# Forgetting attention on one core: softmax sums taken from the transposed weights in heads 0 to 12

## The chip, the cores and the metric

One core of a Trainium2 chip. The metric is device time in microseconds for one execution of the whole program, the median of several runs.

## The reference

Two residual layers and a final RMS norm over x of 1024 positions by 1024 channels, in float32. Layer 0 is a gated linear recurrence (RG-LRU). Layer 1, which the change touches, is attention with a forget gate, 16 heads of 64 channels, in blocks of 128 queries:

```
logits = jnp.einsum("bqhd,bkhd->bhqk", q_blk, kf) * scale
logits = logits + (cq_blk[..., :, None] - ck[:, :, None, :])
logits = jnp.where(mask[None, None], logits, NEG_INF)
p = jax.nn.softmax(logits, axis=-1)
return jnp.einsum("bhqk,bkhd->bqhd", p, vf)
```

`cum` (above `cq_blk` and `ck`) is the running sum of log-sigmoids of the forget logits. The result is multiplied by a SiLU gate and projected out.

## The kernel before

**Number format.** Every float32 product is made of three TensorE matmuls on a high and a low part (`to_hi`, `to_lo`, lines 75 to 86): the high part is the value rounded to the type of TensorE's faster float32 mode, the low part the rest. The helpers `gemm_steps` (lines 111 to 113) and `weights` do this for all projections.

**Stages.** Up to about 460 us layer 0 runs: projections, convolution, scan, output projection. Then the 16 heads of layer 1 follow one another in the loop of line 910. The projections that a later pair of heads needs (queries and keys by `kq_units`, gates by `g_units`, values by `values`) and, from head 13 on, the output projection (`partial`) serve as `fill`: single steps of them are put between the steps of the attention, so that TensorE has work while the others prepare its operands.

**One head.** Queries are treated in two halves of 512 columns, c = 0 and 1. Two generators work on a head:

- `maxima(hd, c)` makes the logits with queries on the partitions, one block of 128 queries after another, in the PSUM tile S (two buffers of two banks). Each stretch of columns takes two matmuls that accumulate: line 656 with the mixed high and low parts (128 rows), line 657 with 96 rows that hold one product of the parts and the forget sums. VectorE adds the causal mask and takes the row's negative maximum in one instruction (line 661); ScalarE takes the exponential in place and its row sum (line 664). The maxima are transposed (L668) and written as four rows of the operand U (L669).
- `weigh(hd, c)` makes the logits again, transposed, with keys on the partitions (lines 723 and 724, tile ST with the same PSUM tag as S); the maxima are now already in the operands, so ScalarE's exponential (729, 732) gives the weights `p`. GpSimd zeroes what the causal mask forbids (737), VectorE splits `p` into `ph` and `pl` (helper lines 81 and 86), and TensorE multiplies them by the values into O (757, 758). ScalarE and VectorE fold the two halves of O into `yo` (762, 763).

After the second half of `maxima` the sums are doubled, inverted and transposed (680 to 685), written to DRAM (686) and read back, spread over 64 partitions, as `recb` (690). `scale(hd)` multiplies the gate by it on GpSimd (699). For odd heads `gated(hd, c)` multiplies `yo` of the pair by that (772), and stores it (778), to be read again (808) as the input of the output projection.

**Order.** The function `run` goes through a string: a digit takes the next step of `weigh` (0) or `maxima` (1), a dot a step of the fill. The first string of a head joins `weigh(hd, 0)` with `maxima(hd, 1)`, the second `weigh(hd, 1)` with `maxima(hd + 1, 0)`:

```
run(first, weigh(hd, 0), maxima(hd, 1), fill=fill, side=side)
scale(hd)
gated(hd, 0)
run(second, weigh(hd, 1), maxima(hd + 1, 0), fill=fill, side=side)
gated(hd, 1)
```

The order in the source is a priority: the planner (`schedule_with_timeline_sim`) plays the program through once at build time and fixes from it the order on each engine's queue, SP's DMA queue among them. On the chip each queue goes in that order. Line 938 loads the operands T and U of head hd + 2 by eight DMAs (`load`: six for the parts of queries and keys, of which the change exchanges two sources, and two for the forget sums).

Tiles come from pools with few buffers: `p`, `ph`, `pl` and `yo` have two, `recb` one, the tag `xp` three (used by the loads of `y` and by `partial`), the PSUM tag O two (O itself, the transposed maxima and the transposed sums).

## Time and profile before

| | |
|---|---|
| time, three runs | 1174.61, 1177.04, 1177.36 us; median 1177.04 |
| the profiled execution | 1181.24 us; its span 1179.5 us |
| TensorE matmuls busy | 1145.0 us, 97% |
| VectorE busy | 830.9 us, 70% |
| ScalarE busy | 594.7 us, 50% |
| GpSimd busy | 404.4 us, 34% |
| mean granted TensorE clock | 0.981 |

All times of instructions come from the one profiled execution. The span is from its first to its last instruction. Busy shares are averages over stages with different limits; a busy TensorE is not TensorE at its peak, as the records of successive matmuls overlap. What a matmul costs in a stream is the distance from its start to the next one's. In a row of instructions, `S<-T,U` says that tile S is written from T and U, and the time in brackets is idle time of the engine before the row, with what ended it.

### The profile page before, as it was taken

What the parts mean: (1) busy time and instruction counts of PE and PEld (TensorE: products, weight loads), DVE (VectorE), ACT (ScalarE), POOL (GpSimd) and SP (SyncE); (2) the same over time, 40 slices, a digit from 0 to 9 for tenths busy, and PEclk for the clock granted to TensorE, in tenths of its full rate; (3) what the DMA queues carried; (4) which work ended last, traced back from release to release, by engine and by line L of the source; (5) the groups of instructions that cost most, each with busy time, mean ns of one, the idle gap of its engine ahead of it and who ended that gap; (6) DMA issues with size and microseconds to landing.
All of it is one profiled execution on the core that took longest, in us unless ns stands there. A gap on an engine that the chain in (4) does not pass through costs nothing.

```text
span 1179.5 us, 15836 instructions
## 1 busy us (share of the span) xinstructions
PE 1145.0 (97%) x5653; PEld 958.7 (81%) x5653; DVE 830.9 (70%) x1272; ACT 594.7 (50%) x1010; POOL 404.4 (34%) x367
## 2 busy tenths in 40 slices
PE   8998999999999999999999999999999999998996
PEld 7786888888888877978888988789888898786895
DVE  7588946766567679666877767777577775675766
ACT  8277453454543757354554545445454454435343
POOL 1223333333323332332343332333333233234345
PEclk8999999999999999999999999999999999998996
DMA  6111111111112214541343413433234332756434
GB/s 207 50 41 31 59 45 46 53 49 41 54 32 59 63 45 138 133 120 56 91 117 75 106 63 91 118 84 88 63 90 109 91 82 61 194 151 199 139 117 143
DMA packets 63278, 105.95 MB, mean 90 GB/s; under 512 B 8856, under 2 KB 27928, under 8 KB 63200
## 3 DMA queue, kind: packets, MB, share of 16 engines
q1 hardware_dynamic: 63200, 104.95, 31.9%
q8 instruction: 44, 0.72, 0.3%
q14 instruction: 34, 0.28, 0.1%
HBM read 63.30 MB, written 16.45 MB: 68 GB/s over the span
## 4 chain that ended last, share of the span: by engine, by line
PE 81%; DVE 9%; DMA 3%; ACT 3%; issue 2%; POOL 1%; SPq 0%; DVEq 0%; ACTq 0%; POOLq 0%
PE gps L111 10%; PE gps L112 10%; PE gps L113 10%; PE ops L113 5%; PE ops L111 5%; PE ops L112 4%; PE ups L111 4%; PE ups L113 4%; PE ups L112 4%; PE ST L723 3%; PE O L758 3%; PE ST L724 3%; PE O L757 2%; PE S L657 2%; PE S L656 2%; PE vps L519 2%
## 5 line engine op out<-in xcount | busy, mean ns | idle before, releaser
L86 POOL TENSOR_TENSOR wl<-wf,wh 128x512 fp32r<-128x512 f32 (+2 forms) x154 | 223.6, 1458 | 409.1 <-ACT wh L75 370.0
L111 PE MATMUL gps<-hh,wh 128*128 128x512 f32 x576 | 227.2, 395 | 0.7 <-DVE qkl L557 0.7
L113 PE MATMUL gps<-hl,wh 128*128 128x512 f32 x576 | 227.1, 394 | 0.0
L112 PE MATMUL gps<-hh,wl 128*128 128x512 f32 x576 | 227.1, 394 | 0.0
L75 ACT CAST wh<-wf 128x512 fp32r<-128x512 f32 (+2 forms) x156 | 93.4, 606 | 118.6 <-PE gps L113 34.1
L664 ACT ACTIVATE S<-S,st 128x128 f32<-128x128 f32 (+7 forms) x128 | 91.4, 714 | 113.6 <-DVE st L661 106.4
L81 DVE CAST ph<-p 128x512 fp32r<-128x512 f32 (+2 forms) x130 | 87.1, 680 | 61.6 <-ACT p L729 31.6
L113 PEld LDWEIGHTS gps<-hl,wh 128*128 128x128 f32 x576 | 108.7, 189 | 24.3 <-issue 0.2
L111 PEld LDWEIGHTS gps<-hh,wh 128*128 128x128 f32 x576 | 108.9, 189 | 21.9 <-DVE qkl L557 1.1
L112 PEld LDWEIGHTS gps<-hh,wl 128*128 128x128 f32 x576 | 108.9, 189 | 21.5 <-POOL wl L86 0.3
L737 POOL TENSOR_SCALAR_AFFINE_SELECT p<-p 128x128 f32<-128x128 f32 (+1 forms) x128 | 48.0, 393 | 203.4 <-ACT p L732 104.2
L86 DVE TENSOR_TENSOR pl<-p,ph 128x512 fp32r<-128x512 f32 (+2 forms) x130 | 115.1, 902 | 2.3
L661 DVE CUSTOM_DVE_ANT_0 S<-S,mask 128x128 f32<-128x128 f32 (+7 forms) x128 | 96.6, 758 | 6.7 <-PE S L657 5.7
L351 DVE TENSOR_TENSOR x<-x,ops 128x512 f32<-128x512 f32 x80 | 53.6, 681 | 41.5 <-PE ops L113 41.3
L111 PE MATMUL ups<-hh,wh 128*128 128x512 f32 x192 | 77.9, 406 | 4.0 <-ACT hh L77 2.0
L113 PE MATMUL ups<-hl,wh 128*128 128x512 f32 x192 | 77.3, 403 | 0.1
L112 PE MATMUL ups<-hh,wl 128*128 128x512 f32 x192 | 77.0, 401 | 0.0
L729 ACT ACTIVATE p<-ST 128x512 f32<-128x512 f32 (+1 forms) x68 | 53.1, 786 | 44.2 <-PE ST L724 39.0
L519 PE MATMUL vps<-wh,hh 128*128 128x256 f32 (+1 forms) x256 | 72.9, 286 | 0.2 <-DVE qkl L557 0.2
L521 PE MATMUL vps<-wl,hh 128*128 128x256 f32 (+1 forms) x256 | 72.5, 285 | 0.4 <-POOL wl L86 0.4
L520 PE MATMUL vps<-wh,hl 128*128 128x256 f32 (+1 forms) x256 | 72.8, 285 | 0.0
L656 PE MATMUL S<-T,U 128*128 128x256 f32 (+2 forms) x192 | 68.5, 359 | 2.8 <-ACT S L664 2.8
(193 smaller groups left out, 2633.9 us busy)
## 6 DMA issues: line engine op xcount, KB each, us to landing
wf<-in_w SPq DMA_DIRECT2D x100, 256.0 KB
wf<-in_wo SPq DMA_DIRECT2D x64, 128.0 KB
T<-qkh SPq DMA_DIRECT2D x28, 256.0 KB
U<-qkh SPq DMA_DIRECT2D x28, 256.0 KB
x<-in_xt SPq DMA_DIRECT2D x16, 256.0 KB
x1d<-x SPq DMA_DIRECT2D x16, 256.0 KB
wf<-in_wv SPq DMA_DIRECT2D x16, 256.0 KB
xp<-x1d SPq DMA_DIRECT2D x16, 256.0 KB
```

Of the source, the lines that this page charges most:

```text
L75: nc.scalar.copy(hi, src)
L81: eng.tensor_copy(hi, src)
L86: return eng.tensor_tensor(lo, src, f32(hi), ALU.subtract)
L111: nc.tensor.matmul(o, wh, xh[:, cs], start=i == 0, stop=False)
L112: nc.tensor.matmul(o, wl, xh[:, cs], start=False, stop=False)
L113: nc.tensor.matmul(o, wh, xl[:, cs], start=False, stop=i == len(pairs) - 1)
L519: nc.tensor.matmul(pt, xh, wh, start=k == 0, stop=False)
L520: nc.tensor.matmul(pt, xl, wh, start=False, stop=False)
L521: nc.tensor.matmul(pt, xh, wl, start=False, stop=k == KT - 1)
L656: nc.tensor.matmul(S[:, lo_:hi_], U[s][:, 0, qs], T[s][:, 0, lo_:hi_], start=True, stop=False)
L661: nc.vector.tensor_tensor_reduce(S[:, :n], S[:, :n], mask[:, SEQ - n :], -1.0, -NEG, ALU.add, ALU.min, accum_out=m)
L664: nc.scalar.activation(S[:, :n], S[:, :n], AF.Exp, bias=f32(m), scale=-1.0, accum_out=sums[:, i : i + 1])
```

## The change

For heads 0 to 12 (`hd < LIGHT`):

- `maxima` makes only the second of its two matmuls. `load` exchanges the low and the high part of the queries in U, so that this one now holds the product of the high parts with the forget sums. The maximum of these rougher logits is only a shift that cancels between weights and sums.
- The exponential of the untransposed logits and its row sum go.
- `weigh` adds up the masked weights `p` over the blocks of keys in an accumulator `acc` on VectorE (tag `xp`), and at the end of each half four float32 matmuls with a column of ones sum it over the partitions; VectorE copies the four columns to the place where ScalarE's sums stood.
- The inversion of the sums (now the function `inverse`) comes after the second half of `weigh`, and `scale` and `gated(hd, 0)` come after the second `run`.

For all heads the high part of `p`, where no column of the step is masked, is now made by ScalarE instead of VectorE.

```
-                nc.sync.dma_start(f32(A[:64, 0, cs]), hi)
+                nc.sync.dma_start(f32(A[:64, 0, cs]), hi if is_k else lo)
...
-                    nc.sync.dma_start(f32(A[:64, 1, cs]), lo)
+                    nc.sync.dma_start(f32(A[:64, 1, cs]), hi)
...
-                    nc.tensor.matmul(S[:, lo_:hi_], U[s][:, 0, qs], T[s][:, 0, lo_:hi_], start=True, stop=False)
                     last[0] = nc.tensor.matmul(
-                        S[:, lo_:hi_], U[s][:96, 1, qs], T[s][:96, 1, lo_:hi_], start=False, stop=True
+                        S[:, lo_:hi_], U[s][:96, 1, qs], T[s][:96, 1, lo_:hi_], start=True, stop=light
                     )
+                    if not light:
+                        last[0] = nc.tensor.matmul(
+                            S[:, lo_:hi_], U[s][:, 0, qs], T[s][:, 0, lo_:hi_], start=False, stop=True
+                        )
...
-                nc.scalar.activation(S[:, :n], S[:, :n], AF.Exp, bias=f32(m), scale=-1.0, accum_out=sums[:, i : i + 1])
+                if not light:
+                    nc.scalar.activation(
+                        S[:, :n], S[:, :n], AF.Exp, bias=f32(m), scale=-1.0, accum_out=sums[:, i : i + 1]
+                    )
...
+            if not light and (hd == HEADS - 1 or c == 1):
+                inverse(hd, 4 * c if hd == HEADS - 1 else 0, 4 * c + 4)
...
+            acc = at.tile([P, HALF], F32, tag="xp", name="acc", bufs=3) if hd < LIGHT else None
...
-                    to_hi(ph[:, sl, :n], p[:, sl, :n], nc.vector)
+                    to_hi(ph[:, sl, :n], p[:, sl, :n], nc.vector if masked else nc.scalar)
...
+                if acc is not None:
+                    d = [q - begin for q in qlo]
+                    if j0 == 0:
+                        if d[1]:
+                            nc.vector.tensor_copy(acc[:, : d[1]], p[:, 0, : d[1]])
+                        nc.vector.tensor_tensor(acc[:, d[1] :], p[:, 0, d[1] :], p[:, 1, : ns[1]], ALU.add)
+                    else:
+                        for jj in range(2):
+                            a_ = acc[:, d[jj] :]
+                            nc.vector.tensor_tensor(a_, a_, p[:, jj, : ns[jj]], ALU.add)
...
+            if acc is not None:
+                col = ps.tile([P, HALF], F32, tag="O", name="sums")[:, :4]
+                for b in range(4):
+                    nc.tensor.matmul(
+                        col[:, b : b + 1], acc[:, b * P : (b + 1) * P], onesf[:, :1], start=True, stop=True
+                    )
+                nc.vector.tensor_copy(stats[hd][1][:, 4 * c : 4 * c + 4], col)
+                if c == 1:
+                    inverse(hd, 0, 8)
+                yield
...
-            scale(hd)
-            gated(hd, 0)
+            if hd >= LIGHT:
+                scale(hd)
+                gated(hd, 0)
             run(second, weigh(hd, 1), maxima(hd + 1, 0), fill=fill, side=side)
             drain(side)
+            if hd < LIGHT:
+                scale(hd)
+                gated(hd, 0)
             gated(hd, 1)
```

40 lines of the change are left out of this document (22 added, 18 removed).

## The prediction

> **What bounds the kernel now.** I read the page first (busy shares, the chain of waits), then the windows by stage, then the timelines of single engines.
>
> ```profile
> span 1179.5 us, 15836 instructions
> ...
> PE 1145.0 (97%) x5653; PEld 958.7 (81%) x5653; DVE 830.9 (70%) x1272; ACT 594.7 (50%) x1010; POOL 404.4 (34%) x367
> ...
> PE 81%; DVE 9%; DMA 3%; ACT 3%; issue 2%; POOL 1%; SPq 0%; DVEq 0%; ACTq 0%; POOLq 0%
> ```
>
> TensorE (PE) is busy for 97% of the span and holds 81% of the chain that ended last; VectorE (DVE) is next with 70% and 9%. ScalarE (ACT), from which the change takes most work, holds 3% of the chain. These are averages, so the stage of heads 0 to 12 is looked at by itself (columns: window, its length, then busy us of PE, weight loads, DVE, ACT and POOL, granted clock, DMA share, GB/s):
>
> ```profile
> 553.00:972.00 419.00, 415.64 (x2249) 358.21 (x2248) 308.51 (x578) 209.99 (x430) 146.53 (x162) 1.00 0.36 90
> 583.00:615.00 32.00, 31.14 (x154) 26.01 (x153) 25.73 (x46) 17.30 (x36) 14.82 (x15) 1.00 0.47 115
> 615.00:646.00 31.00, 30.94 (x153) 25.79 (x152) 24.62 (x45) 15.87 (x32) 8.69 (x12) 1.00 0.34 79
> ```
>
> From 553 to 972 us PE is idle for 3.4 us of 419 (419.00 less 415.64), at full granted clock. DVE has 74% of this stage (308.51 of 419), and 79 to 80% in heads where no value projection dilutes it (24.62 of 31, 25.73 of 32). So in this stage time is the sum of PE's start-to-start intervals. ACT is idle for 46 to 50% of it (17.30 of 32 busy, 209.99 of 419), and taking work from it gives nothing by itself.
>
> **Change, term 1: the pass of untransposed logits that goes (PE).** The form of each row below: start, duration, instruction. A matmul's slot is the distance to the next start, since durations overlap.
>
> ```profile
> 597.48 0.28 PE L656 MATMUL S<-T,U 128*128 128x256 f32 x1
> 597.60 0.29 PE L657 MATMUL S<-T,U 96*128 96x256 f32 x1
> ...
> 602.38 0.40 PE L656 MATMUL S<-T,U 128*128 128x512 f32 x1
> 602.62 0.40 PE L657 MATMUL S<-T,U 96*128 96x512 f32 x1
> 602.85 0.34 PE L656 MATMUL S<-T,U 128*128 128x384 f32 x1
> 603.03 0.34 PE L657 MATMUL S<-T,U 96*128 96x384 f32 x1
> ```
>
> A slot is 0.235 us for 512 columns (602.38 to 602.85 is two), 0.18 for 384 (602.85 to 603.03), 0.12 for 256 (597.48 to 597.60); I estimate 0.15 for 320, between the last two. By the loop of `maxima` a head has five matmuls of 512 in a pass, two of 384, two of 320 and three of 256: 1.175 + 0.36 + 0.30 + 0.36 = 2.2 us. For 13 heads: 28.5 us less on PE.
>
> **Term 2: the sums of the transposed weights that come (PE).** Each half of a head gets four matmuls of one column, with a 128x128 block of the float32 accumulator as weights. The norm's column sums have this form already:
>
> ```profile
> 458.09 1.84 PE L133 MATMUL sscol<-onesf,sq 128*128 128x1 f32 x16
> 459.80 0.48 PE L111 MATMUL gps<-hh,wh 128*128 128x512 f32 x1
> 460.11 0.40 PE L425 MATMUL ops<-yh,wh 128*128 128x512 f32 x1
> ```
>
> In the code that is eight matmuls (four blocks, two parts), and the row has 16 records, two for each. They hold PE for 1.71 us (458.09 to 459.80), 0.107 us a record, although each has one column to stream: their price is not their width. The matmul behind them takes a slot of 0.31 us and not 0.235, 0.08 more. A group of four is thus 8 x 0.107 + 0.08 = 0.935 us, and 26 groups (13 heads, two halves) come to 24.3 us. Terms 1 and 2 leave PE with only 4.2 us less.
>
> The Trainium skill ("TensorE: Matmul & The Clock Gate", section "LDWEIGHTS") puts a weight load at columns over 1.2 GHz, an estimate of 107 ns for 128, and the row agrees to the nanosecond. The same page's section "Back-to-back issue gap" gives a matmul of 1 to 64 columns about 25 ns, by which the 208 records would cost an estimated 5 us; the row, with a new weight for every record, speaks against that.
>
> **Term 3: VectorE and ScalarE (off PE's path, if they stay under it).**
>
> ```profile
> L664 ACT ACTIVATE S<-S,st 128x128 f32<-128x128 f32 (+7 forms) x128 | 91.4, 714 | 113.6 <-DVE st L661 106.4
> ```
> ```profile
> L86 DVE TENSOR_TENSOR pl<-p,ph 128x512 fp32r<-128x512 f32 x69 | 50.7, 735 | 1.5
> L81 DVE CAST ph<-p 128x1024 fp32r<-128x1024 f32 x30 | 41.2, 1374 | 31.0 <-ACT p L729 31.0
> L664 ACT ACTIVATION_READ_ACCUMULATOR S<-S,st 128x1 f32 x128 | 24.8, 194 | 0.1
> L75 ACT CAST xch<-xc 128x1024 fp32r<-128x1024 f32 x12 | 12.6, 1050 | 54.3 <-DVE xc L265 54.3
> L685 DVE COPY rc<-tr 8x128 f32<-8x128 f32 x15 | 4.2, 277 | 10.7 <-PE tr L683 10.7
> ```
>
> ACT loses eight exponentials a head with their accumulator reads, 8 x (0.714 + 0.194) = 7.3 us, and gets two casts of 1024 columns, 2 x 1.05 = 2.1 us. DVE gets ten adds a head over 3,840 columns in all (896 in the first half, 2,944 in the second); at the 0.735 us of a 512-column subtraction of the same kind that is 5.5 us, and with three small copies at 0.277 it is 6.3 us. It loses two casts at 1.374, 2.75 us. Net it gains 3.6 us a head, so 25.73 becomes 29.3 of 32 us and 24.62 becomes 28.2 of 31: 91%. It stays under PE, and the adds are urgent for nobody but the two-buffer tile `p` and the end of the half, so I cost them at nothing on the path; without that cover it is 3.6 us a head less the 6.3 us of idle DVE time. The logit tile S leaves its PSUM buffer after the maximum instead of after the exponential, which helps PE. PE's own waits between 535 and 985 us (sum, times, longest):
>
> ```profile
> PE O L758 <- DVE pl L86: 3.2, 3, 1.3
> ```
> ```profile
> PEld ST L723 <- ACT S L664: 1.7, 7, 0.3
> ```
>
> They are three for `pl`, 3.2 us together, and the weight loads' queue waited 1.7 us for S, held by ScalarE. The three `pl` waits have a cause that the change moves:
>
> ```profile
> 588.75 2.39 POOL L699 TENSOR_TENSOR sg<-sg,recb 64x1024 f32<-64x1024 f32 x1 [3.55 <-ACT yo L762]
> 591.22 1.62 POOL L86 TENSOR_TENSOR wl<-wf,wh 128x512 fp32r<-128x512 f32 x1
> 592.80 2.27 POOL L772 TENSOR_TENSOR yo<-yo,sg 128x512 f32<-128x512 f32 x1
> 595.02 1.43 POOL L737 TENSOR_SCALAR_AFFINE_SELECT p<-p 128x128 f32<-128x128 f32 x4
> ```
> ```profile
> 586.57 1.22 DVE L86 TENSOR_TENSOR pl<-p,ph 128x1024 fp32r<-128x1024 f32 x1
> ...
> 591.73 2.20 DVE L86 TENSOR_TENSOR pl<-p,ph 128x1024 fp32r<-128x1024 f32 x1
> ```
>
> The same subtraction takes 1.22 us with GpSimd idle and 2.20 us beside its 591.22 and 592.80. Now the scaling moves out of the half with the widest tiles, so I take half of the 3.4 us of idle PE as gained: 1.7, between nothing and all of it. The Trainium skill ("SBUF — State Buffer", section "SBUF: two separate sides") states that a DVE instruction with two SBUF inputs and a reading GpSimd instruction exclude each other on a shared port pair. The 2.20 agrees in kind, and by that rule the ten adds would also hold up the masks.
>
> **Term 4: what moves.** For heads 0 to 12 the reciprocal, its two DMAs, `scale` and the first `gated` (with its store) go from the middle of the head to its end, ahead of the load of head hd+2 on SP's queue and of the next head's masks on POOL's. Scale and two gated products are 2.39 + 2.27 + 2.27 = 6.9 us of POOL in a row at the end of an odd head. I cost this at nothing because PE has projection matmuls there; the rival below prices the loss of that cover. The reordered high and low parts in `load` are the same eight DMAs: nothing.
>
> **Term 5: the accumulators share the buffers "xp"**, which before were free until head 13, so that three loads of `y` went out early:
>
> ```profile
> 604.06 0.34 SPq L808 DMA_DIRECT2D y<-y1d  x1
> ...
> 1008.73 9.03 SPq L808 DMA_DIRECT2D y<-y1d  x6
> ```
> ```profile
> 1014.25 0.62 ACT L75 CAST yhh<-y 128x512 fp32r<-128x512 f32 x1 [4.51 <-DMA y<-y1d]
> ```
>
> A load costs the queue 1.5 us (9.03 over 6) and ScalarE already waits 4.51 us for one. Between none and three of them (4.5 us) become late; I take one, +1.5 us, as the last accumulator of head 12 is the only one held to the end.
>
> **Sum.** -28.5 + 24.3 - 1.7 + 1.5 = -4.4 us, against the profiled execution of 1181.24 us, 1.7 above its own span and 4.2 above the median of 1177.04. From the median: 1172.6 us. A measurement of this kernel tells about 0.3%, 3.5 us, from no change, so the forecast stands just beyond that.
>
> **Rivals.**
>
> *GpSimd's end-of-head chain stalls PE (slower).* If the next head's masks stand behind scale and gated in POOL's order while these wait for the reciprocals, the splits and then the output matmuls come late at each of 13 transitions. By the row of three waits one costs 1.07 us: 13.9 us, and with terms 1, 2 and 5 it is 1177.0 - 2.7 + 13.9 = 1188 us. It decides once the chain from column sum to masks is longer than the projection work beside it. A wait near 2 us costs double:
>
> ```profile
> 1023.80 0.50 PE L723 MATMUL ST<-U,T 128*128 128x512 f32 x1 [1.90 <-ACT S L664]
> ...
> 1026.14 0.63 PE L112 MATMUL ops<-yhh,wl 128*128 128x512 f32 x1
> 1026.57 0.63 PE L113 MATMUL ops<-yhl,wh 128*128 128x512 f32 x1
> ```
>
> Behind that wait the slots are 0.43 us (1026.14 to 1026.57) for a while, at half the speed. For it: waits for the reciprocals end much of POOL's idle time. Against: the same chain in the middle of the head cost PE three waits in twelve heads.
>
> *DVE becomes the bound (slower).* If the adds meet GpSimd as the 2.20 us row does, 5.5 us a head becomes 9.9 (x 1.8), and 24.62 + 3.6 + 4.4 = 32.6 us exceeds the 31 of the head. In seven even heads that is 1.6 us each, 11 us, and 1184 us after term 1 and 2. Against: GpSimd is busy for only 8.69 us of those 31.
>
> *All idle time goes (faster).* S is free earlier and ACT is nearly empty: -4.2 - 3.4 = -7.6, 1169.4 us; if the wait at 1023.80 with its slow slots (1.9 + about 2) is replanned away too, 1165.5.
>
> *The cheap sums (faster).* If the sums' weight loads hid under the neighbouring matmuls they would cost next to nothing: up to 28.5 us, 1149. The 16 records in a row with 0.107 each speak against it; the skill's 25 ns sentence above is its only support.
>
> *It gives nothing.* A tile S that takes half as long to make waits for DVE's maximum, and the 4.2 us come back as such waits: 1177.
>
> **How the numbers follow.** Forecast (PE's difference decides, ends from -8 to 0 us): 0.50. POOL chain 0.17, DVE 0.10, nothing gained 0.08, idle time gone 0.12, cheap sums 0.03. Faster by over 0.3% (under 1173.5): 0.31 of the forecast's 0.50, with 0.12 and 0.03: 0.46. Slower (over 1180.6): most of 0.17 and 0.10, 0.24. The rest, 0.30, within. Range: from 1165 (idle time gone) to 1187 (just short of the POOL chain in full); 2 in 10 outside. The likeliest case's own range is 1169 to 1177.
>
> **What would show it.** Right: 156 fewer matmuls at the S line, 208 more records of one column at 0.107 us slots in groups of eight; DVE near 84% from 553 to 972 us (308.5 + 12 x 3.6 over 419), ACT near 35% (210.0 - 12 x 5.2); PE's idle time in that stage no greater than 3.4 us. Wrong: output or column-sum matmuls waiting for DVE by 1 us and more at the ends of heads; masks on POOL that follow scale and gated immediately; a half-speed stretch inside heads 0 to 12; column sums at slots under 0.05 us.

## The result, and the profile after

The changed kernel takes 1196.63 us, the median of four runs (1194.78 to 1199.61), beside 1177.2 us of the kernel before (four runs, 1174.61 to 1178.74): a ratio of 1.0168, with a 95% interval from 1.0145 to 1.019. It is slower by 19.4 us, where 4.4 less was forecast, and it lies above the predicted range, which ended at 1187 us. Its profiled execution took 1196.33 us, 15.1 more than the profiled one of before.

The page of the changed kernel: span, busy shares, the chain that ended last, and the group of adds.

```profile
span 1194.6 us, 15842 instructions
...
PE 1143.5 (96%) x5705; PEld 952.0 (80%) x5705; DVE 880.4 (74%) x1406; ACT 543.3 (45%) x837; POOL 405.6 (34%) x367
...
PE 72%; DVE 15%; issue 5%; DMA 3%; ACT 2%; POOL 2%; SPq 0%; DVEq 0%; POOLq 0%; ACTq 0%
...
L785 DVE TENSOR_TENSOR acc<-acc,p 128x256 f32<-128x256 f32 (+1 forms) x104 | 74.7, 718 | 4.4 <-POOL p L754 3.2
```

TensorE's records went from 5653 to 5705, which is 156 less and 208 more, as the change says, and its busy time fell by 1.5 us. VectorE gained 49.5 us (880.4 less 830.9). TensorE's share of the last chain fell from 81% to 72% and VectorE's rose from 9% to 15%, and of VectorE's lines the page names only the adds. So the time was not added to TensorE's work; it went into TensorE waiting for VectorE, and into a lower clock behind these waits. The windows by stage show where (columns as before). First the kernel before, in the stretch from 538 to 1015 us, which holds heads 0 to 12:

```profile
538.00:1015.00 477.00, 473.64 (x2532) 407.01 (x2531) 341.16 (x636) 234.50 (x479) 164.32 (x181) 1.00 0.36 89
```

and the changed kernel, over the same stretch, the predicted stage, three parts of its first heads, and two parts around the first bad place:

```profile
538.00:1015.00 477.00, 461.24 (x2483) 392.20 (x2482) 383.75 (x756) 172.86 (x295) 158.99 (x174) 0.98 0.33 83
553.00:985.00 432.00, 416.24 (x2245) 353.48 (x2244) 357.49 (x703) 153.56 (x259) 142.26 (x159) 0.98 0.34 84
573.00:611.00 38.00, 36.35 (x179) 29.54 (x178) 35.16 (x69) 13.63 (x21) 11.97 (x15) 1.00 0.31 71
611.00:642.00 31.00, 27.61 (x126) 21.82 (x125) 24.77 (x44) 9.04 (x15) 11.39 (x11) 0.94 0.40 103
642.00:675.00 33.00, 32.41 (x210) 29.07 (x209) 30.13 (x59) 13.47 (x24) 8.24 (x11) 1.00 0.33 73
611.60:618.00 6.40, 5.86 (x33) 4.78 (x32) 1.50 (x5) 1.10 (x2) 1.38 (x1) 1.00 0.22 65
617.96:637.60 19.64, 16.79 (x76) 12.91 (x75) 19.20 (x30) 7.12 (x12) 9.23 (x9) 0.96 0.45 112
```

TensorE was idle for 3.4 us of the 477 before and is for 15.8 now (477.00 less 461.24), 12.4 more. The granted clock fell from 1.00 to 0.98. In windows of 1 us it is 0.50 in four stretches of 3.4, 3.4, 6.8 and 3.4 us, from 567.7, 636.0, 786.2 and 939.8 us on, and 1.00 elsewhere: 17.1 us at half speed, or 8.5 us of work that was not done. These two, less the 4.2 us by which terms 1 and 2 were to shorten the work, make 16.7 us.

VectorE's load is 83% of the stage (357.49 of 432), but it is not spread evenly. From 573 to 611 us it is 93% (35.16 of 38). That work does not pile up into the next head: from 611.6 to 618.0 VectorE is busy for 1.50 of 6.40 us, as it waits for TensorE and ScalarE. From 618 to 637.6 it is busy for 19.20 of 19.64 us, and there the first long stall lies (611 to 642: 3.4 us idle in 31, at a clock of 0.94). From 642 to 675 VectorE is at 91% and TensorE loses 0.6 us only, so a full VectorE alone does not make a stall; it depends on what stands in its queue.

The loss grows with the heads. The 2nd, 10th, 18th and 26th writing of the maxima into U on VectorE start at 546.5, 679.6, 832.6 and 982.9 us by the timeline, and before at 549.4, 678.1, 824.0 and 969.4: 2.9 us ahead, then 1.5, 8.6 and 13.5 behind. Between the first and the last of these four the changed kernel loses 16.4 us, which the 16.7 above account for. TensorE's own waits in heads 0 to 12 (sum, times, longest):

```profile
PE O L774 <- DVE ph L82: 4.4, 6, 0.8
PE sums L796 <- DVE U L679: 3.9, 7, 0.7
PE S L660 <- DVE st L668: 2.0, 4, 0.6
PE O L774 <- DVE sums L799: 1.3, 3, 0.4
```

All four name VectorE. The second is that of the new column sums, and it is named for U, not for an add: their PSUM tile has the tag O with two buffers, and one of them is held by the transposed maxima until VectorE has written U from them. The fourth is O waiting in its turn for the copy of the sums. No wait for VectorE is over 0.83 us. The timeline of TensorE at the first bad place (start, duration, instruction, idle time before it):

```profile
629.60 0.54 PE L660 MATMUL S<-T,U 96*128 96x320 f32 x2
630.87 0.50 PE L774 MATMUL O<-ph,v 128*128 128x512 f32 x1 [0.74 <-DVE ph L82]
...
632.03 0.50 PE L775 MATMUL O<-pl,v 128*128 128x512 f32 x1 [0.32 <-DVE pl L87]
...
633.77 0.38 PE L774 MATMUL O<-ph,v 128*128 128x256 f32 x1 [0.83 <-DVE ph L82]
634.82 1.05 PE L796 MATMUL sums<-onesf,acc 128*128 128x1 f32 x8 [0.67 <-DVE U L679]
635.73 0.55 PE L738 MATMUL ST<-U,T 128*128 128x512 f32 x1
...
637.57 0.63 PE L113 MATMUL gps<-hh,wl 128*128 128x512 f32 x1
638.00 0.63 PE L114 MATMUL gps<-hl,wh 128*128 128x512 f32 x1
```

and VectorE's at the same time:

```profile
628.09 1.30 DVE L785 TENSOR_TENSOR acc<-acc,p 128x384 f32<-128x384 f32 x1
629.32 0.69 DVE L497 TENSOR_TENSOR gps<-gps,rs 128x512 f32<-128x512 f32 x1
629.92 1.26 DVE L82 CAST ph<-p 128x512 fp32r<-128x512 f32 x2
631.10 1.34 DVE L87 TENSOR_TENSOR pl<-p,ph 128x512 fp32r<-128x512 f32 x2
632.37 0.41 DVE L785 TENSOR_TENSOR acc<-acc,p 128x256 f32<-128x256 f32 x1
632.71 0.68 DVE L558 SCALAR_TENSOR_TENSOR qkl<-gps,qkh 128x512 fp32r<-128x512 f32 x1
633.31 0.41 DVE L82 CAST ph<-p 128x512 fp32r<-128x512 f32 x1
633.64 0.41 DVE L785 TENSOR_TENSOR acc<-acc,p 128x256 f32<-128x256 f32 x1
634.08 0.68 DVE L679 TENSOR_TENSOR U<-mrow,own 4x512 fp32r<-4x512 f32 x1
```

No row of VectorE has idle time in brackets: it works through a backlog. The split that TensorE waits for at 633.77 starts at 633.31, behind an add of 0.41 us and a projection's low part; the split before, at 629.92, stands behind an add of 1.30 us and a projection's eviction. In a queue that goes in order, an add for which nobody waits delays the next one for which somebody does. The last add ends at 634.05 and U at 634.76, and the column sums start at 634.82: U released them. The four waits in brackets come to 2.56 us, and behind them a matmul of 512 columns takes 0.43 us (637.57 to 638.00), half speed, until about 639.4. The same picture stands at 782 to 793 and at 934 to 943 us; at 567.7 us half speed follows 0.6 us of waits.

The other waits can be followed in the same way. Of TensorE's 15.8 us of idle time, 13.8 us are 27 waits that end on an instruction of VectorE. Take the rows of VectorE's timeline from its last idle time up to that instruction: in 24 of the 27, 12.2 us, the adds among these rows are longer than the wait. The other three, of 0.54 us each (the first at 614.95), have no add in front of U. Without the adds these instructions could have started earlier by more than the wait, if their own inputs were there, which was not followed up for each.

### The profile page after: what moved, and what is told of

Read it like the earlier page. It is cut to its first block, busy times and chain, and to the rows that moved or that the text cites. A ratio compares the mean times of both kernels' runs of the same rounds, so it can differ in the third digit from the quotient of the medians.

```text
span 1194.6 us, 15842 instructions
## 1 busy us (share of the span) xinstructions
PE 1143.5 (96%) x5705; PEld 952.0 (80%) x5705; DVE 880.4 (74%) x1406; ACT 543.3 (45%) x837; POOL 405.6 (34%) x367
## 4 chain that ended last, share of the span: by engine, by line
PE 72%; DVE 15%; issue 5%; DMA 3%; ACT 2%; POOL 2%; SPq 0%; DVEq 0%; POOLq 0%; ACTq 0%
PE gps L112 8%; PE gps L113 8%; PE gps L114 8%; PE ops L112 5%; PE ops L113 5%; PE ops L114 5%; PE ups L114 3%; PE ups L112 3%; PE ups L113 3%; DVE acc L785 3%; PE S L660 2%; PE vps L520 2%; PE O L775 2%; PE vps L522 2%; PE vps L521 2%
## 5 line engine op out<-in xcount | busy, mean ns | idle before, releaser
L754 POOL TENSOR_SCALAR_AFFINE_SELECT p<-p 128x128 f32<-128x128 f32 (+1 forms) x128 | 54.8, 443 | 238.8 <-ACT p L747 142.7
L87 DVE TENSOR_TENSOR pl<-p,ph 128x512 fp32r<-128x512 f32 (+2 forms) x130 | 117.9, 915 | 6.4 <-ACT ph L76 5.6
L785 DVE TENSOR_TENSOR acc<-acc,p 128x256 f32<-128x256 f32 (+1 forms) x104 | 74.7, 718 | 4.4 <-POOL p L754 3.2
L774 PE MATMUL O<-ph,v 128*128 128x512 f32 (+1 forms) x198 | 69.0, 350 | 6.0 <-DVE ph L82 4.6
L738 PE MATMUL ST<-U,T 128*128 128x512 f32 (+1 forms) x198 | 69.3, 359 | 4.2 <-ACT S L672 3.4
```

Source lines behind the costliest of these rows:

```text
L87: return eng.tensor_tensor(lo, src, f32(hi), ALU.subtract)
L738: nc.tensor.matmul(A[:, jj, :n], T[s][:, 0, ks], U[s][:, 0, q0:end], start=True, stop=False)
L774: nc.tensor.matmul(o, v, ph[:, jj, : ns[jj]], start=j == 0, stop=False)
L785: nc.vector.tensor_tensor(a_, a_, p[:, jj, : ns[jj]], ALU.add)
```

## The experiments

Three theories were weighed at first. **A**: the adds make VectorE late for everything behind them. **B**: the moved chain (reciprocals, their two DMAs, `scale`, `gated`) holds GpSimd and so the masks. **C**: the column sums, in TensorE's own queue, hold it while they wait for the adds. Two more were formed on the way. **Y**: the late first `gated` keeps the tile `yo` and holds ScalarE. **D**: the column sums hold TensorE while they wait for their PSUM buffer. Line numbers are those of the changed kernel where it is the base. The planner runs anew for each kernel, so an edit can also change the order of all queues; where the orders were compared, in the traces, the text says so.

| kernel | base and edit | median us | ratio to the kernel before (95%) |
|---|---|---|---|
| the changed kernel | | 1196.63 | 1.0168 (1.0145 to 1.019) |
| e1 | changed, adds of line 785 gone | 1177.88 | 0.9995 (0.9978 to 1.0011) |
| e2 | e1, column matmuls gone too | 1211.05 | 1.0297 (1.0262 to 1.0332) |
| e3 | before, chain moved, nothing else | 1214.8 | 1.0319 (1.0284 to 1.0353) |
| e5 | changed, all splits' casts on ScalarE | 1189.07 | 1.0099 (1.0071 to 1.0126) |
| e6 | changed, `yo` free early | 1197.67 | 1.0174 (1.0147 to 1.0201) |
| e7 | e5 and e6 | 1190.03 | 1.0116 (1.0091 to 1.0141) |
| e8 | e7, column sums of half the records | 1184.11 | 1.0065 (1.0041 to 1.0088) |
| e9 | before, unmasked casts on ScalarE | 1174.31 | 0.9981 (0.9966 to 0.9997) |
| e10 | changed, unmasked adds on GpSimd | 1208.08 | 1.0276 (1.0236 to 1.0316) |
| e11 | e8 and e10 | 1185.7 | 1.0074 (1.0058 to 1.009) |
| e12 | changed, each add of line 785 twice | 1234.49 | 1.0497 (1.0478 to 1.0516) |
| e13 | before, one pass alone | 1159.76 | 0.9858 (0.9842 to 0.9874) |
| e14 | e13 and e9 | 1157.13 | 0.9826 (0.9806 to 0.9845) |
| e15 | e13 and all casts on ScalarE | 1161.88 | 0.9861 (0.9833 to 0.989) |
| e16 | changed, column sums of constant ones | 1189.72 | 1.0094 (1.0073 to 1.0115) |
| e17 | changed, column sums in O's columns | 1205.8 | 1.0245 (1.0223 to 1.0267) |
| e18 | changed, column sums in the projections' tag | 1222.99 | 1.0392 (1.0368 to 1.0415) |
| e19 | e16 and e17 | 1204.78 | 1.0239 (1.0219 to 1.0258) |

### e1: without the adds

```
-                    else:
-                        for jj in range(2):
-                            a_ = acc[:, d[jj] :]
-                            nc.vector.tensor_tensor(a_, a_, p[:, jj, : ns[jj]], ALU.add)
```

The copy and the add that open each half (lines 780 and 781) stay, so the column matmuls still follow the masks of that step. Eight adds a head go (the expectation counts nine), and the sums leave out the later key blocks.

> The changed kernel without nine of the ten adds a head into the accumulator: only the first add of each half stays, so the sums leave out the later key blocks (1 is added to them so that the reciprocal stays finite). All matmuls, casts, DMAs and their places stay. Theory A (VectorE's queue is the new bound: the adds stand in front of the splits and evacuations that TensorE waits for): about 4.7 us a head leave VectorE, the waits go, and the time falls to 1170 to 1175 us. Theory B (the reciprocals, scale and gated moved to the head's end stall TensorE by way of GpSimd): 1190 us or more. Theory C (TensorE is held by the column sums themselves): 1188 us or more.

Measured: 1177.88 us, 18.7 below the changed kernel and level with the kernel before. The stage by the windows:

```profile
538.00:1015.00 477.00, 470.48 (x2589) 404.91 (x2588) 337.08 (x677) 182.03 (x310) 158.95 (x181) 1.00 0.36 89
```

The clock is back at 1.00, TensorE's idle time down to 6.5 us, VectorE down to 71%. The adds carry the loss, by their time, by what waits for them, or by the order that the planner makes around them. The moved chain is in this kernel as well, and costs little in its order. The order on TensorE differs from the changed kernel's from the first column sums on.

### e2: without the adds and without the column matmuls

```
-                    nc.tensor.matmul(
-                        col[:, b : b + 1], acc[:, b * P : (b + 1) * P], onesf[:, :1], start=True, stop=True
-                    )
-                nc.vector.tensor_copy(stats[hd][1][:, 4 * c : 4 * c + 4], col)
+                nc.vector.tensor_copy(stats[hd][1][:, 4 * c : 4 * c + 4], acc[:, :4])
```

> As the run without adds, and the eight column-sum matmuls a head go too (a copy of four columns of the accumulator stands in their place, so the sums mean nothing). Beside the run without adds this prices the column sums. Theory A: 22 to 25 us less than the run without adds, about 1148 to 1152 us. Theory C: 35 us less than it or more, as the waits behind the sums go with them. Theory B: about 1167 to 1172 us.

Measured: 1211.05 us. It has 208 records less than e1 and is 33 us slower, which no sum of costs gives. GpSimd's waits from 553 to 985 us name what is late:

```profile
POOL sg L713 <- DMA recb<-recd: 102.8, 12, 12.4
```

In e1 the same wait comes to 42.4 us and in the changed kernel to 26.1. This run was meant to price the column sums, and doesn't. e3, which has the same kind of wait, shows what such an order looks like.

### e3: the chain moved, and nothing else

```
-            if hd == HEADS - 1 or c == 1:
+            if hd >= LIGHT and (hd == HEADS - 1 or c == 1):
...
-            scale(hd)
-            gated(hd, 0)
+            if hd >= LIGHT:
+                scale(hd)
+                gated(hd, 0)
             run(second, weigh(hd, 1), maxima(hd + 1, 0), fill=fill, side=side)
             drain(side)
+            if hd < LIGHT:
+                inverse(hd, 0, 8)
+                scale(hd)
+                gated(hd, 0)
```

In the source `inverse` stands here behind the whole second `run`; in the changed kernel it stands inside it, at the end of `weigh(hd, 1)`.

> The kernel before with one part of the change alone: for heads 0 to 12 the inversion of the sums with its two DMAs, scale and the first gated come after the second run of the head. Two matmuls, exponential and ScalarE's sums stay. Theory A: 1174 to 1181 us, no change that can be told. Theory B: 1188 us or more.

Measured: 1214.8 us, 37 above the kernel before, with the same number of instructions on each engine. SP's queue at the end of head 1:

```profile
594.11 1.35 SPq L574 DMA_DIRECT2D U<-qkl  x1
595.56 1.20 SPq L692 DMA_DIRECT2D recd<-rc  x1
596.80 1.26 SPq L575 DMA_DIRECT2D T<-cumd  x1
...
599.44 0.47 SPq L696 DMA_DIRECT2D recb<-recd  x1
```

GpSimd's queue:

```profile
603.02 2.36 POOL L704 TENSOR_TENSOR sg<-sg,recb 64x1024 f32<-64x1024 f32 x1 [11.64 <-DMA recb<-recd]
605.46 0.54 POOL L742 TENSOR_SCALAR_AFFINE_SELECT p<-p 128x128 f32<-128x128 f32 x2
```

and TensorE's:

```profile
606.33 0.50 PE L762 MATMUL O<-ph,v 128*128 128x512 f32 x1 [2.19 <-DVE ph L82]
```

The reciprocals' DMAs stand between the eight loads of T and U, GpSimd waits 11.64 us in front of `scale`, the masks of the next head come right behind it, and the output matmul waits 2.19 us for the split of the masked weights. That is rival 1 as the prediction described it, in a kernel that loses over two and a half times its price of 13.9 us. But it is not what the changed kernel does. There, at the same transition, SP issues the reciprocals' DMAs at 611.61 and 613.04, when the loads' last went out at 598.46, and GpSimd does the masks at 607.09 ahead of `scale` at 616.62. e1 has that order too:

```profile
600.51 0.26 SPq L701 DMA_DIRECT2D recd<-rc  x1
601.71 0.47 SPq L705 DMA_DIRECT2D recb<-recd  x1
```

So the moved chain costs between little and 37 us, by the place that the planner gives to its DMAs and masks. That each of e3's 37 us comes through this chain was not shown; that the order of the queues differs, and not the work, was.

### e5 and e9: the casts to ScalarE

```
-                    to_hi(ph[:, sl, :n], p[:, sl, :n], nc.vector if masked else nc.scalar)
+                    to_hi(ph[:, sl, :n], p[:, sl, :n], nc.vector if masked and hd >= LIGHT else nc.scalar)
```

is e5. e9 puts the changed kernel's own version of this line, the one with a minus, into the kernel before.

> The changed kernel with ScalarE making every high part of the weights p in heads 0 to 12, the masked ones too: six casts a head, about 2.8 us, leave VectorE, and ScalarE, busy 45%, takes them at 0.6 us each. Theory A: about half of the loss comes back, 1182 to 1189 us. Theories B and C: 1193 to 1199 us, unchanged.

> The kernel before with one part of the change alone: ScalarE makes the high part of p where no column is masked. 26 casts of 1.37 us leave VectorE in heads 0 to 12. Theory A: VectorE at 74% is no bound in the kernel before, 1174 to 1179 us, at most the 3 us of waits for the low parts gained. A gain of over 4 us would say that VectorE already set TensorE's pace before the change.

Measured: e5 1189.07, 7.6 us better than the changed kernel, with VectorE at 847.5 us and not 880.4. e9 1174.31, a ratio of 0.9981: the casts that the change moves are worth some 2 us where VectorE isn't full. Here 33 us of other work than the adds leave VectorE, and 7.6 come back, which speaks for A.

### e6 and e7: the tile yo

```
+            g_ = sgs[pair][:, c * HALF + sub.start : c * HALF + sub.stop]
+            to = g_ if hd < LIGHT else yo
-            nc.gpsimd.tensor_tensor(
-                yo, yo, sgs[pair][:, c * HALF + sub.start : c * HALF + sub.stop], ALU.mult
-            )
+            nc.gpsimd.tensor_tensor(to, yo, g_, ALU.mult)
...
-                nc.sync.dma_start(y1d[c, pair], yo)
+                nc.sync.dma_start(y1d[c, pair], to)
```

> The changed kernel in which, for heads 0 to 12, gated writes its product into the gate's tile and stores it from there, so that yo is free after GpSimd's product and not after the store. In the changed kernel's profile ScalarE's copy into yo waits five times for the store, 11.2 us in all, with exponentials queued behind it, just ahead of the stalls of heads 2, 6 and 10. Theory Y (the late gated keeps yo, ScalarE stands, TensorE starves): these waits go and with them most of the stalls of those three heads, 1180 to 1186 us. Theory A (VectorE's backlog with the adds in it): 1193 to 1199 us.

> The same, and ScalarE makes all high parts of p in heads 0 to 12 (that alone gave 1189 us). Theory Y: 1173 to 1179 us. Theory A: 1186 to 1191 us.

Measured: 1197.67 and 1190.03 us, each within 1.1 us of its base. ScalarE's waits for the store of `yo` come to 11.2 us in the changed kernel; e6 has 3.8 us instead, for GpSimd's product. Theory Y fell: the wait shrank by two thirds and the time did not move. The order on TensorE is that of the changed kernel, instruction by instruction, up to 996 us, and VectorE's differs by a few exchanges, so this comparison is clean.

### e8: column sums of half the records

The accumulator gets TensorE's faster float32 type, and the column of ones becomes two columns, so that each matmul is one record and not two:

```
+            acc = at.tile([P, HALF], F32R, tag="xp", name="acc", bufs=3) if hd < LIGHT else None
...
-                        col[:, b : b + 1], acc[:, b * P : (b + 1) * P], onesf[:, :1], start=True, stop=True
+                        col[:, 2 * b : 2 * b + 2], acc[:, b * P : (b + 1) * P], onesr, start=True, stop=True
```

> The run before this one, and the accumulator is held in the rounded type of the faster float32 mode, so that a column sum is one weight load and matmul of two columns instead of two of one: 104 records fewer. If TensorE's slots set the time, 10 to 12 us less than that run. If VectorE's backlog sets it, 0 to 4 us less.

Measured: 1184.11 us, 5.9 below e7. At 0.107 us the 104 records that go would be 11.1 us. It lies between the theories and decides nothing alone; where the other half went, no run shows.

### e10 and e11: the adds on GpSimd

```
-                            nc.vector.tensor_tensor(a_, a_, p[:, jj, : ns[jj]], ALU.add)
+                            (nc.vector if masked else nc.gpsimd).tensor_tensor(a_, a_, p[:, jj, : ns[jj]], ALU.add)
```

and the same for the add of line 781. e11 has this edit on e8.

> The changed kernel with the three adds a head of the unmasked steps (512 columns each, 0.93 + 2 x 0.79 us in its profile) on GpSimd instead of VectorE. Theory A (VectorE's backlog): a quarter to a half of the loss comes back, 1186 to 1192 us. If not VectorE's load but the order of the plan or the wait of the column sums sets the time: 1194 to 1200 us. If GpSimd, with some 6 us a head more, makes the masks late: over 1200 us.

> The run with the short column sums (1184 us), and the three unmasked adds a head on GpSimd as well. Theory A: 1174 to 1180 us, about the kernel before or a little under it. Otherwise 1182 to 1188 us.

Measured: e10 1208.08 us, 11 worse than the changed kernel, and e11 1185.7, no better than e8. One group of e10 and TensorE's first two waits:

```profile
L785 POOL TENSOR_TENSOR acc<-acc,p 128x512 f32<-128x512 f32 x26 | 43.1, 1657 | 17.3 <-ACT p L744 16.4
```
```profile
PE O L774 <- DVE ph L82: 7.9, 5, 2.4
PE O L775 <- DVE pl L87: 5.9, 9, 1.7
```

An add of 512 columns takes 1657 ns on GpSimd and 793 on VectorE, and there it stands ahead of the masks (at 623.84 and 625.35, with masks at 625.09 and 626.60). TensorE waits longer for the splits than in the changed kernel although VectorE has 27 us less to do. A queue with room on average is no free place either, if what everybody waits for goes through it.

### e12: each add twice

```
                             nc.vector.tensor_tensor(a_, a_, p[:, jj, : ns[jj]], ALU.add)
+                            nc.vector.tensor_tensor(a_, a_, p[:, jj, : ns[jj]], ALU.add)
```

> The changed kernel with each of the eight adds a head that accumulate done twice, so that the sums count the later key blocks double: 75 us more of VectorE in heads 0 to 12, nothing else. Theory A, VectorE the bound in most of the stage: 45 to 75 us more, 1240 to 1270 us. If the adds only matter by their place in the plan: 1195 to 1215 us.

Measured: 1234.49 us, 37.9 more than the changed kernel. The page:

```profile
PE 1163.1 (94%) x5705; PEld 964.1 (78%) x5705; DVE 916.7 (74%) x1510; ACT 544.4 (44%) x837; POOL 416.3 (34%) x367
```

This lies between the two ranges. VectorE's busy time rose by 36.3 us in all (916.7 less 880.4; the new adds are 62.1, and other rows became shorter) and the kernel by 37.9, about as much; TensorE's waits for `pl` alone are 11.6 us in heads 0 to 12. Between e1 and the changed kernel 59.7 us of VectorE (880.4 less 820.7) made 18.7, about one for three. By this row of four (e1, e5, the changed kernel, e12) time rises with VectorE's load, first a part of it and at the end all. That is A's picture, with the planner's order as an unknown in each point: e16 and e17, below, have the changed kernel's load within 4 us, and take 6.9 us less and 9 more. So the load alone does not set the time.

### e16: the column sums without their wait

```
-                        col[:, b : b + 1], acc[:, b * P : (b + 1) * P], onesf[:, :1], start=True, stop=True
+                        col[:, b : b + 1], onesf, onesf[:, :1], start=True, stop=True
```

All adds and all column matmuls are made, but the matmuls take a constant tile, so that they don't wait for the adds.

> The changed kernel in which the column-sum matmuls take a constant tile of ones as weights instead of the accumulator: the sums are a constant and mean nothing; adds, matmuls, copies, inversion and DMAs all stay, but no matmul waits for an add. Theory A (VectorE's load): 1190 to 1198 us, little changed. Theory C (the column sums wait for the adds in TensorE's queue and hold up what is behind them): 1175 to 1183 us.

Measured: 1189.72 us, 6.9 below the changed kernel, with VectorE as busy as there (877.9 us by its page). TensorE's waits for the column sums:

```profile
PE sums L796 <- DVE U L679: 1.6, 5, 0.3
```

Taken alone this looks like 6.9 us for C. But from the third group of column sums on (579 us) the orders on TensorE differ. Half speed lasts 10.2 us from 538 to 1015 here, against 17.1, which is 3.4 of the 6.9 us. And the changed kernel's own trace speaks against C: before each of its seven waits of column sums, the last add ended at least 0.7 us earlier than the U that ended the wait. No column sum of that kernel was held for an add; what e16 gains by the rest of its order was not shown any further.

### e17, e18, e19: the column sums' PSUM buffer

e17 writes the sums into the tile O that the half has just given up, e18 takes a buffer from the projections, e19 is e17 on e16:

```
-                col = ps.tile([P, HALF], F32, tag="O", name="sums")[:, :4]
+                col = O[:, :4]
```
```
-                col = ps.tile([P, HALF], F32, tag="O", name="sums")[:, :4]
+                col = ps.tile([P, HALF], F32, tag="g", name="sums")[:, :4]
```

> The changed kernel with the column sums written into the first four columns of the tile O that the half has just given up, instead of into a PSUM tile of their own; all work is as in the changed kernel. Theory D: TensorE's waits before the column sums (3.9 us, all ended by VectorE's U) are not for the adds but for a buffer of the PSUM tag O, which the transposed maxima hold until VectorE has written U, because the sums are a third tenant of two buffers. Then these waits go, those of O for the copied sums and of the maxima for yo (1.3 and 0.9 us) shrink, and with the half-speed slots behind them the kernel takes 1188 to 1192 us. Theory C (the sums wait for the adds): 1195 to 1199, and the waits before the sums stay at 3 us or more with the accumulator or U as their end. Theory A alone (VectorE's load): 1195 to 1199 too, waits for ph unchanged at 4 us.

> The changed kernel with the column sums' PSUM tile in the tag of the projections (two buffers, emptied by VectorE and ScalarE) instead of that of O; all work is as in the changed kernel. Theory D: the buffer of O no longer matters, but a projection's tile is held for the sums and their copy instead: 1188 to 1196 us, with new waits of projection matmuls for the copied sums under 2 us in all. Theories A and C: 1195 to 1200 us.

> As e17, and the column matmuls take a constant tile of ones instead of the accumulator, so they wait neither for the adds nor for a buffer of their own; the softmax's sums are constants, all adds are made. Theory D: no further gain over e17, 1188 to 1192 us, since the wait was for the buffer. Theory C: e16's gain again or more, 1185 to 1190, at least 5 us under e17. Theory A: what stays above 1178, some 10 us, is VectorE's load, and waits for ph, pl and st remain.

Measured: 1205.8, 1222.99 and 1204.78 us. All three are slower than every range above, and the planner is why they decide less than they were made for. e17 and e19 have one order on every queue up to 1030 us, so through heads 0 to 12. e18 has another from the first column sums on (543 us), and so has e17 beside the changed kernel: in e17 the sums can't be written before O is folded into `yo`, and stand later.

e19 against e17 is 1.0 us, within the intervals: in this order the column sums' waiting for the adds costs next to nothing. The trace of e17 has a single wait before them, 0.3 us. The first wait of TensorE in e17, in heads 0 to 12:

```profile
PE ST L739 <- DVE U L679: 3.7, 6, 0.8
```

It is as long as the 3.9 us before the column sums were, and for the same U: with the sums out of the way, the next matmul that reads U waits in their place. D's gain did not come, but D is not disproved for the changed kernel's own order. There the 0.9 us of a group of column sums could run while U is awaited, if the sums had a buffer; no run tests it. Its waits before the sums (3.9 us) and of O for the copied sums (1.3), with their share of the half speed, bound what D can be worth. Where no add was in the way, VectorE's row at 614 us shows that U itself waited for the transposed maxima from TensorE:

```profile
614.21 0.68 DVE L679 TENSOR_TENSOR U<-mrow,own 4x512 fp32r<-4x512 f32 x1 [1.47 <-PE mrow L678]
```

e18 is 17 us slower than e17, in another order, so this is no price of the buffer. Its largest waits of TensorE:

```profile
PE O L775 <- DVE pl L87: 11.2, 12, 2.2
PE gps L112 <- DVE qkl L558: 5.4, 5, 1.3
```

The second is that of projection matmuls for a buffer that VectorE empties: the projections, which are to fill TensorE's time while it waits for VectorE, now wait for it too. VectorE has 74% of the stretch from 538 to 1015 us there (353.01 of 477), less than the 80% of the changed kernel.

### e13, e14, e15: one pass, the sums left on ScalarE

The kernel before with the exchange in `load` and only this in `maxima`:

```
-                    nc.tensor.matmul(S[:, lo_:hi_], U[s][:, 0, qs], T[s][:, 0, lo_:hi_], start=True, stop=False)
                     last[0] = nc.tensor.matmul(
-                        S[:, lo_:hi_], U[s][:96, 1, qs], T[s][:96, 1, lo_:hi_], start=False, stop=True
+                        S[:, lo_:hi_], U[s][:96, 1, qs], T[s][:96, 1, lo_:hi_], start=True, stop=hd < 13
                     )
+                    if hd >= 13:
+                        last[0] = nc.tensor.matmul(
+                            S[:, lo_:hi_], U[s][:, 0, qs], T[s][:, 0, lo_:hi_], start=False, stop=True
+                        )
```

The exponential, its sums and the chain stay where they were; in heads 0 to 12 the sums are now those of the rougher logits, made of the product of the high parts alone, while the weights are of the full ones. e14 adds e9's edit, e15 e5's.

> The kernel before with one part of the change alone: heads 0 to 12 make the untransposed logits in one pass (with the parts of the queries exchanged in load); exponential and ScalarE's sums stay and are taken of these rougher logits. By TensorE's slots, 28.5 us less: 1146 to 1152 us. If VectorE or the other engines set the pace once TensorE has less to do: 1155 to 1165 us. If TensorE's slots were not what set the time before: 1170 us or more.

> The kernel before with the one-pass logits in heads 0 to 12 (that alone gave 1160 us; ScalarE's sums are of these rougher logits) and ScalarE making the high part of p where no column is masked: 26 casts leave VectorE in those heads. If VectorE holds the missing 11 us: 1148 to 1156 us. If the waits behind S and ScalarE's exponential hold them: 1157 to 1163 us.

> The same with all six casts a head of heads 0 to 12 on ScalarE (masked steps too; the unmasked ones of heads 13 and 14 stay on VectorE): ScalarE, busy 51% in the one-pass run, comes to about 60 to 65%. If VectorE's load holds the missing time: a little under the run before this one, 1145 to 1154 us. If ScalarE's queue becomes the bound instead: 1160 us or more.

Measured: 1159.76, 1157.13 and 1161.88 us. e14 is faster than both kernels, by 1.7% (0.9826, from 0.9806 to 0.9845). The removed pass alone gives 17.3 us of the 28.5 that its slots are worth. e13's stage and two waits in it:

```profile
553.00:955.00 402.00, 387.59 (x2071) 329.60 (x2069) 311.56 (x571) 206.05 (x423) 148.62 (x162) 1.00 0.37 94
```
```profile
PE ST L726 <- ACT S L667: 7.1, 4, 1.9
PE O L761 <- DVE pl L86: 4.4, 4, 1.2
```

TensorE is idle for 14.4 us there (402.00 less 387.59), 11 more than in the whole stage before: the first wait is for the tile S, which ScalarE's exponential holds, as TensorE now comes back for it earlier. e14 has 4.8 us of such waits in heads 0 to 12, ten of at most 0.9 us. e15 takes still more from VectorE and gains nothing, so VectorE's load isn't what bounds e13. Why e14's casts help is open; another order from the planner would do.

## Why the prediction was wrong

**What bounds the kernel: right.** TensorE was the bound of before, and e13 shows it: matmuls taken from it shorten the kernel.

**Terms 1 and 2: the counts and the slots were right.** 156 fewer and 208 more are as expected, and so is the price of the sums once they start. The column sums of head 1, second half, in the changed kernel:

```profile
614.95 1.05 PE L796 MATMUL sums<-onesf,acc 128*128 128x1 f32 x8 [0.54 <-DVE U L679]
615.86 0.48 PE L739 MATMUL ST<-U,T 128*128 128x512 f32 x1
```

Eight records hold TensorE for 0.91 us (614.95 to 615.86), 0.114 a record; 0.935 had been put down for a group with its tail. The rival of cheap sums is out. The account above also closes with terms 1 and 2 at their 4.2 us. What the term left out is that the sums' tile is a third tenant of two PSUM buffers; what that costs in the changed kernel's order is open (its waits come to 3.9 and 1.3 us). The removed pass as a whole is borne out by e13 for 17.3 of its 28.5 us; the rest is lost there to waits for S, which the prediction had listed only under "it gives nothing".

**Term 3: the load was right, and "I cost them at nothing on the path" was the step that failed.** VectorE gained 49.5 us in all, 3.8 a head where 3.6 were forecast; the stage is at 83% where 84 were; ScalarE at 36% (153.56 of 432) where 35 were. The parts were less good: the adds came to 93.8 us, 7.2 a head and not 5.5, mostly for the narrow ones. Two of the groups by shape (count, busy us, mean ns):

```profile
L785 DVE TENSOR_TENSOR acc<-acc,p 128x256 f32<-128x256 f32 x52 | 34.4, 662 | 3.1 <-POOL p L754 2.9
L785 DVE TENSOR_TENSOR acc<-acc,p 128x512 f32<-128x512 f32 x39 | 30.9, 793 | 1.3 <-ACT p L744 0.7 <-POOL p L754 0.3
```

An add of 256 columns took 0.662 us in the mean, and 0.41 where GpSimd was idle (632.37). So did all 35 of the 52 that ran beside no GpSimd instruction; 384 columns took 0.55 and 512 took 0.68 to 0.69 in that case. At these prices the adds would be an estimated 71 us, 5.5 a head, just what was forecast. The other 22 us or so belong to adds that ran beside GpSimd. All else of VectorE's work came out cheaper, and the sum was right by that.

But the conclusion that it "stays under PE" was drawn from an average of 91% a head. It compared loads, where the order in the queue decides. VectorE's work comes in bunches, when splits, maxima, a projection's eviction and the adds meet: VectorE is idle for 4.9 us from 611.6 to 618.0, and then for 0.44 in 19.64, and in that bunch TensorE needs the splits. The sentence that "the adds are urgent for nobody" but the tile `p` and the end of the half looked only at who waits for an add. What stands behind it in VectorE's queue is urgent: the splits for O, U for the column sums, the maxima for S, which are TensorE's waits above. In place of nothing on the path, TensorE's idle time rose by 12.4 us and half speed took 8.5. Without the eight adds of line 785 18.7 us come back (e1), doubled they cost 37.9 more (e12), each in an order of its own. The other guess, that TensorE is held by column sums that wait for adds, fell with the changed kernel's trace and, in another order, with e19.

The Trainium skill ("SBUF — State Buffer", section "SBUF: two separate sides") was quoted for adds and masks excluding each other. Beside other GpSimd instructions the adds agree: one of 256 columns that started at 578.64, beside GpSimd's 578.22 (2.38 us) and 580.57 (1.29 us), took 3.49 us and ended 0.27 us after the second.

**The 1.7 us of idle time taken as gained: wrong in sign.** Idle time went up by 12.4 us. The half-speed slots, which the prediction listed among the signs that would prove it wrong, came in addition, and cost 8.5 us.

**Term 4: right for this kernel, and by luck.** At the transition of head 1 masks went ahead of `scale`, and GpSimd's waits for `recb` fell (from 50.4 to 26.1 us between 553 and 985). Rival 1 happens in e3, where the planner chose another order and the kernel loses 37 us, and by GpSimd's waits for `recb` in e2. The prediction took the order of the source for the order of the queues, in both its term and its rival.

**Term 5: not tested by itself.** ScalarE's waits for the loads of `y` are 14.4 us in all, 11.5 before: 2.9 us more, where 1.5 on the path was put down; whether they lie on the path was not followed.

**The rivals.** "DVE becomes the bound" (0.10, 1184 us) had the right engine. Its condition, that VectorE's work exceeds the head, was too strict: from 611 to 642 us VectorE is busy for 24.77 of 31, and 20 full us within that were enough. It also had no price for the clock. The range ended at 1187 because the sizes of rivals were taken one at a time, each as idle time only.

What stays open: how much of the 18.7 us is VectorE's load and how much the order that the planner made around the adds, since no two kernels with and without adds share an order (e16 and e17, with about the changed one's load, run at 1189.7 and 1205.8 us in other orders); where e13's missing 11 us go beyond its two waits; and why e11 gains nothing on e8.

## What to carry to other kernels

Work that is "urgent for nobody" still stands in an in-order queue: ask what stands behind it and when that is needed, and look at the engine's load in windows of ten or twenty us, where its work comes in bunches, not at its average in the stage. Where a planner fixes the order at build time, an edit's effect is that of the new order too: the same work moved cost 37 us here, so compare the queues' orders in the traces before a difference is put down to the edit, and look for pairs that keep them (e17 and e19 through heads 0 to 12). Taking one part of a change alone (e13, e14) can be worth more than the whole.

## What the runs showed of the hardware that was not expected

**The clock.** Four waits of 0.32 to 0.83 us, 2.56 us in all within 4.7 us, were followed by 3.4 us of matmuls at half speed (0.43 us a slot, from 636.0 to 639.4), and the granted clock from 611 to 642 us is 0.94. A stage with no wait over 0.84 us in it can thus lose 8.5 us to the clock beside 15.8 of idle time. The half-speed stretches of the changed kernel last 3.41, 3.42, 6.83 and 3.41 us by windows of 1 us, and they start 68.3, 150.2 and 153.6 us apart, 20, 44 and 45 times 3.413. The half-speed stretches of e3, e12 and e16 to e19 lie on such grids too, each run on its own. So the clock here is set for 3.41 us at a time; the same waits can fall into one such window or be shared by two. The Trainium skill ("TensorE: Matmul & The Clock Gate", section "What's actually happening") has the clock halved after an idle window of about 3.4 us and free-running windows of that length. The grid agrees. But no window here was idle throughout: before the four stretches TensorE was idle for 0.6, 1.5, 1.3 and 1.4 us of a window. Several short waits are thus enough. Without column sums a window with 1.05 us of idle time was followed by full speed (from 629.2) and one with 1.26 by half (from 782.8); with eight records of column sums in it, 0.54 us were followed by full speed (from 765.7) and 0.59 by half (from 564.3). So the one-column matmuls seem to count in part as idle time, which was not tested by itself.

**Adds beside GpSimd.** An add of 256 columns takes 0.41 us, and up to 3.49 beside GpSimd. Four of the 52 take 13.5 us together.

**Less work, more time.** e2 has 208 matmul records less than e1 and takes 33 us more, with GpSimd's waits for `recb` at 102.8 us and not 42.4: that is the planner's order, not the chip.
